# Modulation vectors of the second FFN: summed around the attention in place of the FFNs before it

## The chip, the cores and the metric

The kernel runs on one core of one Trainium2 chip. The metric is the device time of one execution in microseconds (us). The engines are TensorE (PE in the profile; its weight loads are PEld), VectorE (DVE), ScalarE (ACT), GpSimd (POOL) and SyncE (SP), which here only issues transfers. Each engine runs its own list of instructions in the order in which the built program holds it.

## The reference

Two layers with shared structure act on 640 tokens (512 latent, 128 context) of width 1024. A layer is a half-step FFN, an attention block and another half-step FFN. Every one of the three is modulated by vectors that come from a linear map of the condition:

```
ada = (silu(c) @ w_ada[l] + b_ada[l])             # 9 vectors of 1024 for latent, 9 for context tokens
sh1, sc1, g1, sh2, sc2, g2, sh3, sc3, g3 = split(ada, 9)
x = x + 0.5*g1 * ((silu(h @ w_gate) * (h @ w_up)) @ w_down)      # h = rmsnorm(x)*(1+sc1)+sh1
x = x + g2 * (concat(o_mla, o_diff, o_nat) @ w_out)              # attention, from ONE input product h @ w_in
x = x + 0.5*g3 * ((silu(h @ w_gate2) * (h @ w_up2)) @ w_down2)   # h with sc3, sh3
```

Vectors are numbered 0 to 8 per layer. Numbers 6, 7 and 8 (sh3, sc3, g3) belong to the second FFN of the layer, 3, 4 and 5 to the attention.

## The kernel before, in words

**Stages.** `build` runs, for each of the two layers, `ffn(l, "f1")`, `attention(l)` and `ffn(l, "f2")`. Activations lie transposed, a tile of 128 features by 640 tokens. All products are made in three passes (high part by high part, high by low, low by high), so each weight block must be split first: ScalarE casts the high part, VectorE subtracts to get the low part (`Stream.split`). An FFN makes two pairs of blocks plainly, then ten pairs of gate and up blocks by a seven-product scheme (`seven`), with the down products in five chunks between them.

**The order of the work.** The kernel records instructions in Python program order; a scheduler then orders each engine's list by that order and by the readiness that it models. In the attention a planner (`Plan`, with `Clock`) chooses between chains (scores, softmax, outputs) and bulk work (input products `feat` and `tokmm`) by modelled ready times. The first bulk work is nq0, nk0 and nv0 for token group 0 (columns 0 to 383), then for group 1 (384 to 639). Results land in PSUM banks; a product of `feat` takes one of the two banks of tag `q`, and takes it only when the readers of its last content are done. For nq0 and nk0 the readers are ScalarE's cast and VectorE's subtraction (`split` in `attention`).

**The boundary before the attention.** At the end of `ffn(l, "f1")` the norm of group 0 and of group 1 is applied (`Boundary.norm`, `Norm.apply`): per feature block a multiply by the broadcast norm, a scale and shift, a cast and the subtraction for the low part, mostly on VectorE. That stands right ahead of the attention's first products.

**The background work.** `Background` sums the modulation vectors. A step takes one vector, one of eight feature blocks and one half of the 1024 inputs: a load of 256 KB from `in_ADA` into a tile of 128x512, and two `tensor_tensor_reduce` on VectorE, one for each of the conditions (`ada_step`). In the profile such a reduce is `CUSTOM_DVE_ANT_0` followed by `DVE_READ_ACCUMULATOR2_ANT part<-`; in the instruction order it reads `ISA ... part<-` followed by `ISA part 128x1`. A vector is 16 steps, hence 32 reduces. `open(limit, rate)` puts the vectors up to `limit` on the list, sets the rate, and loads four rows of the condition through SiLU. `tick` adds the rate to a credit and makes a step for each whole unit. An FFN ticks after each of the seven products and each down product; the very first FFN also ticks three times after each plain product (`EARLY`). `require(l, v)` makes steps at once until vector v is there; it stands ahead of the first down product (vector 2 or 8) and at each boundary (the scale). `finish()` makes all steps that are left, at once. It is called in one place, the first line of `attention`:

```
    def attention(l, bound, nbound):
        BG.finish()
```

Of the kernel before, what the change touches and what calls it, by code (L numbers as in the profile page):

```python
# [51 lines left out]

FETCH = 5
EARLY = 3
RATES = 0.517, 0.339, 0.423, 0
LIMITS = (0, 8), (1, 3), (1, 8), (1, 8)

UNITS = "nnnnnnnnddddddddmmmmmmmm"

# [130 lines left out]
class Clock:  # L190
# [42 lines left out]
    def bank(self, tag, tile):  # L233
        b = self.banks[tag]
        if len(b) >= self.BUFS[tag]:
            b.remove(min(b, key=lambda n: self.used.get(n, 1e18)))
        b.append(tile.tensor.name)
        return tile
# [40 lines left out]
class Plan:  # L279
# [18 lines left out]
    def done(self, name):  # L298
        return not self.open.get(name)
# [28 lines left out]
def build(tc, I, O):  # L328
# [31 lines left out]
    def PB(n=512):  # L360

        return clock.bank("q", pp.tile([128, n], F32, tag="q", name=nm("q"), bufs=4 - NP))
# [123 lines left out]
    def mm3(out, a, b, start, stop, skip=False):  # L486
        PE.matmul(out, a[0], b[0], start=start, stop=False, skip_group_check=skip)
        PE.matmul(out, a[0], b[1], start=False, stop=False, skip_group_check=skip)
        PE.matmul(out, a[1], b[0], start=False, stop=stop, skip_group_check=skip)
# [79 lines left out]
    BG = Background()  # L569
# [133 lines left out]
    def hcols(hT, k, c0, c1):  # L703
        return hT[k][0][:, c0:c1], hT[k][1][:, c0:c1]
# [166 lines left out]
    def attention(l, bound, nbound):  # L871
# [21 lines left out]
        def feat(tag, g, name, done):  # L893
            yield ("q",)
            ps = PB(GR[g][1] - GR[g][0])
            for k in range(ND):
                mm3(ps, W.get((l, tag, k)), hcols(hT, k, *GR[g]), k == 0, k == ND - 1)
                yield
            follow(name, done(ps))

        def tokmm(tag, j, width, name, done, bank=PB):
            yield ("q",) if bank is PB else ()
            ps = bank(width)
            for k in range(ND):
                wh, wl = W.get((l, tag, k))
                hh, hl = hcols(hT, k, j * 128, (j + 1) * 128)
                PE.matmul(ps, hh, wh, start=(k == 0), stop=False)
                PE.matmul(ps, hl, wh, start=False, stop=False)
                PE.matmul(ps, hh, wl, start=False, stop=(k == ND - 1))
                yield  # L910
            follow(name, done(ps))

        def follow(name, chain):
            if chain is not None:
                plan.chain(chain, name)
# [32 lines left out]
        def ckv(j):  # L948
            def done(ps):
                if j == 0:  # L950
                    M["kr"] = pu.tile([128, 5, 32], F32, tag="kr", name=nm("kr"), bufs=1)
                    M["ck"], M["ckP"] = HL(), (PQ("ck", F32R), PQ("ck", F32R))
                    M["mc"] = T(256)
                    SP.dma_start(M["mc"], I["mctx"][l])
                A.copy(M["kr"][:, j], ps[:, 128:160])
                if j == 4:
                    plan.chain(kr_rope(), "ckv")
                return post(rms_rows(ps[:, 0:128], 128))

            def post(t):  # L960
                yield (t, "p")
                pt = P1((128,))
                PE.transpose(pt, t, ident)
                h, lo = hcols(M, "ck", 128 + j * 128, 256 + j * 128) if j < 4 else M["ckP"]
                A.activation(h, pt, AF.Identity, scale=kvn(l))
                V.scalar_tensor_tensor(lo, pt, kvn(l), f32(h), ALU.mult, ALU.subtract)
                if j == 4:
                    o = T(128)
                    V.tensor_scalar(o, pt, kvn(l), None, ALU.mult)
                    G.dma_start(O["ckvT"][l], o)  # L970
                    split(M["ck"][0][:, 0:128], M["ck"][1][:, 0:128], M["mc"][:, 0:128])

            return tokmm("ckv", j, 160, "ckv", done)

        def cq(j):
            def done(ps):
                if j == 0:
                    cqT[0], cqT[1] = HL(), HL()
                return post(rms_rows(ps, 256))

            def post(t):
                yield (t, "p")
                pt = P1((2, 128))
                for c in range(2):
                    PE.transpose(pt[:, c], t[:, c * 128:(c + 1) * 128], ident)
                for c in range(2):
                    h, lo = hcols(cqT, c, j * 128, (j + 1) * 128)
                    A.activation(h, pt[:, c], AF.Identity, scale=qn(l, c))
                    V.scalar_tensor_tensor(lo, pt[:, c], qn(l, c), f32(h), ALU.mult, ALU.subtract)

            return tokmm("cq", j, 256, "cq", done)
# [47 lines left out]
        def nq(i, g):  # L1039
            def done(ps):  # L1040
                if g == 0:
                    Qn[i] = HL(S)
                    split(Qn[i][0][:, 0:384], Qn[i][1][:, 0:384], ps, NAT_SCALE)
                else:
                    split(Qn[i][0][:, 384:512], Qn[i][1][:, 384:512], ps[:, 0:128], NAT_SCALE)
                    QPn[i] = PQ(("n", i))
                    A.activation(QPn[i], ps[:, 128:256], AF.Copy, scale=NAT_SCALE)
            return feat(f"nq{i}", g, f"n{i}", done)

        def nk(i, g):  # L1050
            def done(ps):
                if g == 0:
                    K = Kn[i] = HL()
                    split(K[0][:, 0:256], K[1][:, 0:256], ps[:, 0:256])
                    split(K[0][:, 384:512], K[1][:, 384:512], ps[:, 256:384])
                    split(K[0][:, 256:384], K[1][:, 256:384], nkc[:, i * 128:(i + 1) * 128])
                else:
                    K = Kn[i]
                    split(K[0][:, 512:640], K[1][:, 512:640], ps[:, 0:128])
                    KPn[i] = PQ(("n", i))  # L1060
                    A.copy(KPn[i], ps[:, 128:256])
                    G.dma_start(O["nkT"][l, i], KPn[i])
            return feat(f"nk{i}", g, f"n{i}", done)
# [329 lines left out]
        def dqk(tag, t, g):  # L1393
            def done(ps):
                if g == 0:
                    M[tag, t] = T()
                xf = M[tag, t]
                A.copy(xf[:, GR[g][0]:GR[g][1]], ps)
                if g == 0:
                    return  # L1400
                del M[tag, t]
                y = rope(xf)
                pq = PQ(("d", t))
                A.copy(pq, xf[:, 512:640])
                if tag == "dq":
                    hl = HL(S)
                    split(hl[0], hl[1], y, DIFF_SCALE)
                    QPd[t] = pq
                else:
                    hl = HL()  # L1410
                    split(hl[0][:, 128:640], hl[1][:, 128:640], y)
                    split(hl[0][:, 0:128], hl[1][:, 0:128], M["dc"][:, t * 128:(t + 1) * 128])
                    KPd[t] = pq
                    G.dma_start(O["dkT"][l, t], pq)
                M[tag, "hl", t] = hl
            return feat(f"{tag}{t}", g, f"d{t}", done)
# [263 lines left out]
    def first(k):  # L1680
        for d in range(k + 1 if k else 0, min(k + 2, ND)):
            begin(d)
        if k == ND - 1:
            for e in engines:
                e.pin = None
            W.la = LA["ffn"]
            BG.open(LIMITS[0], RATES[0])

# [3 lines left out]
    def lambdas():  # L1692
        for l in range(L):
            li = 0.8 - 0.6 * math.exp(-0.3 * l)
            pr = SM(2)
            tt = T(64).rearrange("p (a k) -> p a k", a=2)
            lv = lamv[:, l].rearrange("p (a b) k -> p a b k", a=2)
            tc.keep_in_program_order(V.tensor_tensor(tt, lv[:, :, 0], lv[:, :, 1], ALU.mult))
            V.tensor_reduce(pr, tt, AX.X, ALU.add)
            A.activation(pr, pr, AF.Exp)  # L1700
            V.tensor_tensor(neglam[:, l:l + 1], pr[:, 1:2], pr[:, 0:1], ALU.subtract)
            V.tensor_scalar(neglam[:, l:l + 1], neglam[:, l:l + 1], -li, None, ALU.add)
            V.tensor_scalar(subg[:, l:l + 1], sub(l), 1.0 - li, None, ALU.mult)

    for l in range(L):
        b2 = Boundary(l, "mix")
        if l:
            BG.open(LIMITS[2], RATES[2])
        ffn(l, "f1", b, b2, None if l else first)
        if l == 0:  # L1710
            lambdas()
        b3 = Boundary(l, "f2")
        attention(l, b2, b3)
        b = Boundary(l + 1, "f1") if l + 1 < L else Boundary(l, "final")
        BG.open(LIMITS[2 * l + 1], RATES[2 * l + 1])
        ffn(l, "f2", b3, b)
# [125 lines left out]
```

## Time and profile before

| | us |
|---|---|
| median of 3 runs | 2736.33 (2736.01 to 2740.82) |
| profiled execution, its own time | 2733.88 |
| span of the profiled execution | 2732.1 |
| PE busy | 2566.5 (94%) |
| PEld busy | 2429.6 (89%) |
| DVE busy | 2019.7 (74%) |
| ACT busy | 1202.0 (44%) |
| POOL busy | 592.9 (22%) |

By the tile names in the timeline, the first FFN lasts to about 525 us, the first attention to about 940, the second FFN to about 1400, the third FFN to about 1850, the second attention to about 2270 and the last FFN to the end. PE's share of 94% is a mean over stages in which it is busy nearly all the time and stretches in which it waits.

### The profile page before, as it was taken

The page shows a single profiled execution, that of the slowest core. Times are in us where ns is not written, and L with a number is a line of the kernel's source. Part 1 is how long each engine was busy: PE and PEld are TensorE (multiplying, and loading weights), DVE is VectorE, ACT ScalarE, POOL GpSimd, SP SyncE. Part 2 cuts the span into 40 slices and gives each one's busy share as a digit, 9 for nine tenths or more (in the row PEclk, how much of TensorE's full clock was granted, in tenths as well). Part 3 has the DMA queues.
Part 4 walks back from the last instruction along what each step waited for, and adds up shares of the span by engine and source line. Part 5 has one row for each costly group of instructions (what it writes and reads, how often), then busy time and mean ns, then how long its engine had stood idle before and what let it go on. Part 6 is the DMA issues. An engine that isn't in the chain of part 4 may idle for free. (4 is left out here: it accounts for less than half of the span.)

```text
span 2732.1 us, 46623 instructions
## 1 busy us (share of the span) xinstructions
PE 2566.5 (94%) x17216; PEld 2429.6 (89%) x17216; DVE 2019.7 (74%) x4542; ACT 1202.0 (44%) x2618; POOL 592.9 (22%) x618
## 2 busy tenths in 40 slices
PE   5799999999989999999999999999988898999998
PEld 5799999977867899999999999998777788999998
DVE  4999999633476799888779999965345669666665
ACT  4333334454366553333453333335445666333441
POOL 0322222012223122222112222301122312222220
PEclk9899999999989999999999999999999899999999
DMA  6376666221321346665436665632213212545441
GB/s 243 119 207 197 199 199 172 95 88 58 93 53 42 117 131 182 172 172 163 140 78 185 197 177 165 182 103 79 89 54 90 54 63 80 144 122 137 123 120 39
DMA packets 144819, 349.73 MB, mean 128 GB/s; under 512 B 18496, under 2 KB 21472, under 8 KB 144592
## 3 DMA queue, kind: packets, MB, share of 16 engines
q1 hardware_dynamic: 119616, 302.28, 34.1%
q0 software_dynamic: 23392, 42.97, 9.6%
q8 instruction: 136, 2.23, 0.3%
q10 hardware_dynamic: 1584, 1.50, 0.2%
q14 instruction: 91, 0.75, 0.1%
HBM read 330.27 MB, written 4.36 MB: 122 GB/s over the span
## 5 line engine op out<-in xcount | busy, mean ns | idle before, releaser
L272 PE MATMUL q<-t,u 128*128 128x320 f32 (+2 forms) x8448 | 1369.3, 315 | 42.9 <-DVE t L272 27.8
L272 PEld LDWEIGHTS q<-t,u 128*128 128x128 f32 x8448 | 1272.2, 191 | 72.8 <-issue 26.0
L272 DVE TENSOR_TENSOR u<-raw,u 128x512 fp32r<-128x512 f32 (+1 forms) x668 | 489.1, 738 | 126.5 <-ACT u L272 80.6
L272 ACT CAST u<-raw 128x512 fp32r<-128x512 f32 (+1 forms) x668 | 400.7, 616 | 362.3 <-PE q L272 150.5
L272 PE MATMUL s<-t,u 128*128 128x320 f32 (+2 forms) x3008 | 515.7, 323 | 24.5 <-ACT u L272 9.2
L272 PEld LDWEIGHTS s<-t,u 128*128 128x128 f32 (+1 forms) x3008 | 450.9, 192 | 44.6 <-ACT t L272 10.5
L272 PE MATMUL p<-t,u 128*128 128x320 f32 (+1 forms) x2936 | 458.8, 315 | 6.0 <-DVE v L272 5.8
L272 PEld LDWEIGHTS p<-t,u 128*128 128x128 f32 (+1 forms) x2936 | 427.4, 186 | 19.5 <-issue 8.6
L272 DVE CUSTOM_DVE_ANT_0 u<-u,u 128x512 f32<-128x512 f32 x512 | 393.0, 771 | 15.8 <-PE q L272 6.1
L272 DVE SCALAR_TENSOR_TENSOR t<-q,adav,t 128x192 f32<-128x192 f32 (+3 forms) x568 | 235.1, 436 | 118.2 <-PE q L272 117.6
L272 POOL TENSOR_TENSOR u<-raw,raw 128x512 f32<-128x512 f32 x78 | 131.5, 1685 | 474.0 <-PE q L272 149.0
L272 ACT CAST u<-u 128x512 fp32r<-128x512 f32 x234 | 144.8, 619 | 194.8 <-PE q L272 83.0
L272 DVE TENSOR_TENSOR u<-u,u 128x512 fp32r<-128x512 f32 (+2 forms) x265 | 194.1, 732 | 43.2 <-PE q L272 11.8
L272 ACT ACTIVATE t<-t 128x320 f32<-128x320 f32 (+2 forms) x168 | 92.4, 553 | 183.5 <-DVE t L272 180.0
L272 POOL DMA_DIRECT2D raw<-in_W x78 | 68.7, 880 | 476.8 <-DVE t L272 186.3
L272 PE MATMUL q<-u,t 128*128 128x256 f32 (+1 forms) x1086 | 152.9, 298 | 18.8 <-ACT u L272 11.5
L272 PEld LDWEIGHTS q<-u,t 128*128 128x128 f32 x1086 | 143.1, 203 | 24.4 <-ACT u L272 13.5
L272 ACT CAST t<-t 128x320 fp32r<-128x320 f32 (+3 forms) x155 | 78.4, 544 | 104.3 <-DVE t L272 102.8
L272 POOL TENSOR_TENSOR u<-u,raw 128x512 f32<-128x512 f32 x78 | 120.3, 1542 | 17.5 <-DVE u L272 7.4
L272 POOL DMA_DIRECT2D u<-in_W x78 | 76.7, 983 | 188.0 <-DMA u<-in_W 54.6
L272 POOL TENSOR_TENSOR sm<-sm,mhalf 128x1 f32<-128x1 f32 (+5 forms) x37 | 33.1, 895 | 380.7 <-DVE sm L272 379.2
L272 DVE TENSOR_TENSOR v<-p,v 128x320 f32<-128x320 f32 x195 | 94.1, 483 | 20.5 <-PE p L272 19.5
(168 smaller groups left out, 2080.3 us busy)
## 6 DMA issues: line engine op xcount, KB each, us to landing
raw<-in_W SPq DMA_DIRECT2D x330, 512.0 KB, 4.0
u<-in_ADA SPq DMA_DIRECT2D x272, 256.0 KB, 4.5
u<-in_W SPq DMA_DIRECT2D x78, 256.0 KB, 4.2
raw<-in_W POOLq DMA_DIRECT2D x78, 256.0 KB, 5.1
u<-in_W POOLq DMA_DIRECT2D x78, 256.0 KB, 5.8
t<-t SPq DMA_DIRECT2D x80, 80.0 KB, 2.1
t<-in_nbias SPq DMA_DIRECT2D x16, 320.0 KB, 5.0
u<-u SPq DMA_DIRECT2D x80, 64.0 KB, 2.0
```

The lines of the kernel that those rows point to most:

```text
L272: r = f(*a, **k)
```

## The change

The limits and rates of the two FFNs that come first in their layer are lowered, so that vectors 6, 7 and 8 of each layer are no longer summed in them. A second table, `BETWEEN`, opens these vectors just before `attention` is called, at 0.2 steps per tick, and the loops of `feat` and `tokmm` in the attention tick once for each of their eight slices.

```
-RATES = 0.517, 0.339, 0.423, 0
-LIMITS = (0, 8), (1, 3), (1, 8), (1, 8)
+RATES = 0.3, 0.339, 0.17, 0
+LIMITS = (0, 5), (1, 3), (1, 5), (1, 8)
+
+BETWEEN = ((0, 8), 0.2), ((1, 8), 0.2)
 ...
             for k in range(ND):                      # feat
                 mm3(ps, W.get((l, tag, k)), hcols(hT, k, *GR[g]), k == 0, k == ND - 1)
+                BG.tick()
                 yield
 ...
                 PE.matmul(ps, hh, wl, start=False, stop=(k == ND - 1))     # tokmm
+                BG.tick()
                 yield
 ...
         b3 = Boundary(l, "f2")
+        BG.open(*BETWEEN[l])
         attention(l, b2, b3)
```

Per layer three vectors move: 48 steps, 96 reduces, 48 loads. The number of steps in all stays.

How the instructions stand. First VectorE's list of the kernel before, at the boundary to the first attention. `p_5992` is the broadcast norm of group 1, `v` and `t` are the tiles of its application, `q_6077` and `q_6106` are the banks of the first two input products (nq0 and nk0, group 0), and `raw` rows are weight splits:

```order
L272 TENSOR_SCALAR v_5989<-ident,sm_5986 128x128 x2
L272 SCALAR_TENSOR_TENSOR u_6103<-q_6077,u_6102 128x384
L272 TENSOR_TENSOR v_5994<-p_5992,t_75 128x256
L272 TENSOR_TENSOR u_6153<-raw_5693,u_6152 128x512
L272 TENSOR_SCALAR v_5995<-v_5994,adav_91 128x128
L272 TENSOR_TENSOR v_6001<-p_5992,t_76 128x256
L272 TENSOR_TENSOR u_6165<-raw_6162,u_6164 128x512
L272 TENSOR_TENSOR t_5729<-v_5995,t_5728 128x256
L272 TENSOR_SCALAR v_6002<-v_6001,adav_91 128x128
L272 TENSOR_TENSOR v_6008<-p_5992,t_77 128x256
L272 TENSOR_TENSOR t_6132<-q_6106,t_6131 128x256
```

The same place now, where the banks of the first two products are `q_6089` and `q_6118`:

```order
L274 TENSOR_SCALAR v_5741<-ident,sm_5738 128x128 x2
L274 TENSOR_TENSOR v_5746<-p_5744,t_75 128x256
L274 TENSOR_SCALAR v_5747<-v_5746,adav_91 128x128
L274 TENSOR_TENSOR v_5753<-p_5744,t_76 128x256
L274 TENSOR_SCALAR v_5754<-v_5753,adav_91 128x128
L274 ISA u_5836,part<-u_5830,u_5818 128x512
L274 ISA part 128x1
L274 TENSOR_TENSOR t_5481<-v_5747,t_5480 128x256
L274 TENSOR_TENSOR v_5760<-p_5744,t_77 128x256
L274 TENSOR_TENSOR t_5489<-v_5754,t_5488 128x256
L274 TENSOR_SCALAR v_5761<-v_5760,adav_91 128x128
L274 TENSOR_TENSOR v_5767<-p_5744,t_78 128x256
```

The readers of the two banks and the two weight splits have left this place, and the first reduce stands in it. All 96 reduces of the layer follow within 224 rows, with the rest of the norm and the eight small rows of `lambdas` between the first of them. After the last reduce VectorE's list goes on so:

```order
L274 ISA u_6064,part<-u_6064,u_5821 128x512
L274 ISA part 128x1
L274 TENSOR_TENSOR t_6144<-q_6118,t_6143 128x256
L274 TENSOR_TENSOR adav_91<-part 128x16
L274 TENSOR_TENSOR adav_91<-adav_91,bada 128x16
L274 TENSOR_SCALAR adav_91<-adav_91 128x16
L274 TENSOR_TENSOR t_6144<-q_6118,t_6143 128x128
L274 TENSOR_TENSOR t_6144<-u_6078,t_6143 128x128
L274 SCALAR_TENSOR_TENSOR u_6115<-q_6089,u_6114 128x384
L274 TENSOR_TENSOR u_6165<-raw_5445,u_6164 128x512
```

The two readers of bank `q_6118`, the reader of `q_6089` and the next weight split now stand behind the 96th reduce. The second layer's list has the same shape at its own boundary: the reader rows of the first two banks stand behind its 96th reduce.

Then TensorE's list now, at the third product that takes a bank of tag `q` (`q_6240`, nq0 for group 1); `s_1262` is a bank of nv0:

```order
L274 MATMUL s_1262_6213<-u_5448,t_5512 128x256
L274 MATMUL s_1262_6213<-u_5447,t_5520 128x256
L274 MATMUL s_1262_6213<-u_5447,t_5521 128x256
L274 MATMUL s_1262_6213<-u_5448,t_5520 128x256
L274 MATMUL q_6240<-t_5480,u_5325 128x256
L274 MATMUL q_6240<-t_5481,u_5325 128x256
L274 MATMUL q_6240<-t_5480,u_5326 128x256
```

In the kernel before, the same product (there `q_6228`) stands behind more work on nv0:

```order
L272 MATMUL s_1258_6201<-u_6152,t_5777 128x256
L272 MATMUL s_1258_6201<-u_6153,t_5776 128x256
L272 MATMUL s_1258_6201<-u_6152,t_5784 128x256
L272 MATMUL s_1258_6201<-u_6152,t_5785 128x256
L272 MATMUL s_1258_6201<-u_6153,t_5784 128x256
L272 MATMUL q_6228<-t_5728,u_5573 128x256
L272 MATMUL q_6228<-t_5729,u_5573 128x256
```

Between the broadcast of the group 1 norm and this product TensorE's list holds 14 products of nk0 and 52 of nv0 before, and 14 and 16 now; the other 36 follow it now. Beyond such places TensorE's list holds the same products in the same order, and GpSimd's list is the same row for row.

## Rows read from the trace of the kernel before

**Rows 1.** The page: the span, then busy time, share and instructions of each engine.

```profile
span 2732.1 us, 46623 instructions
...
PE 2566.5 (94%) x17216; PEld 2429.6 (89%) x17216; DVE 2019.7 (74%) x4542; ACT 1202.0 (44%) x2618; POOL 592.9 (22%) x618
```

**Rows 2.** Windows: stretch, length, PE, PEld, DVE, ACT, POOL busy (count), PEclk, DMA, GB/s.

```profile
100.00:150.00 50.00, 35.66 (x222) 33.96 (x221) 48.76 (x116) 17.47 (x39) 10.94 (x11) 0.86 0.41 128
150.00:450.00 300.00, 292.82 (x1969) 288.46 (x1969) 296.88 (x695) 104.08 (x194) 77.30 (x64) 1.00 0.68 194
...
550.00:750.00 200.00, 185.89 (x1279) 158.93 (x1278) 73.41 (x213) 91.28 (x263) 41.84 (x76) 0.97 0.25 80
1000.00:1350.00 350.00, 345.42 (x2334) 342.12 (x2334) 311.94 (x672) 133.54 (x244) 84.68 (x70) 1.00 0.60 173
...
1450.00:1800.00 350.00, 341.85 (x2300) 338.54 (x2299) 328.24 (x732) 130.65 (x239) 85.65 (x70) 1.00 0.64 181
2310.00:2660.00 350.00, 350.00 (x2389) 350.00 (x2388) 240.48 (x432) 144.00 (x260) 92.20 (x74) 1.00 0.48 127
```

**Rows 3.** The page's costliest groups: the reduces of the modulation vectors.

```profile
L272 DVE CUSTOM_DVE_ANT_0 u<-u,u 128x512 f32<-128x512 f32 x512 | 393.0, 771 | 15.8 <-PE q L272 6.1
```

**Rows 4.** Timeline of VectorE (start, length): four reduces in a row, and what follows.

```profile
122.20 0.68 DVE L272 CUSTOM_DVE_ANT_0 u<-u,u 128x512 f32<-128x512 f32 x1
...
124.65 0.48 DVE L272 TENSOR_TENSOR v<-q,v 128x320 f32<-128x320 f32 x1
```

**Rows 5.** Timeline of VectorE: one of the long reduces.

```profile
316.70 1.79 DVE L272 CUSTOM_DVE_ANT_0 u<-u,u 128x512 f32<-128x512 f32 x1
```

**Rows 6.** Timeline of GpSimd at the time of that reduce.

```profile
316.30 1.63 POOL L272 TENSOR_TENSOR u<-u,raw 128x512 f32<-128x512 f32 x1
```

**Rows 7.** Timeline of VectorE at the start of the first attention.

```profile
534.47 0.42 DVE L272 TENSOR_TENSOR v<-p,t 128x256 f32<-128x256 f32 x1 [0.33 <-PE p L272]
...
536.94 0.34 DVE L272 TENSOR_SCALAR v<-v,adav 128x128 f32<-128x128 f32 x1
537.20 0.41 DVE L272 TENSOR_TENSOR v<-p,t 128x256 f32<-128x256 f32 x1
537.53 0.41 DVE L272 TENSOR_TENSOR t<-q,t 128x256 fp32r<-128x256 f32 x1
...
540.88 0.42 DVE L272 TENSOR_TENSOR t<-v,t 128x256 fp32r<-128x256 f32 x1
541.22 0.34 DVE L272 TENSOR_SCALAR v<-v,adav 128x128 f32<-128x128 f32 x1
```

**Rows 8.** Timeline of TensorE at the start of the first attention.

```profile
534.08 2.80 PE L272 MATMUL q<-t,u 128*128 128x384 f32 x14
536.72 6.63 PE L272 MATMUL s<-u,t 128*128 128x256 f32 x52
543.19 2.08 PE L272 MATMUL q<-t,u 128*128 128x256 f32 x16
```

**Rows 9.** Timeline of TensorE at the start of the second attention.

```profile
1863.04 6.63 PE L272 MATMUL s<-u,t 128*128 128x256 f32 x52
1869.51 5.92 PE L272 MATMUL q<-t,u 128*128 128x256 f32 x48
```

**Rows 10.** Timeline of VectorE there: the first multiply of group 1's norm.

```profile
1860.79 0.42 DVE L272 TENSOR_TENSOR v<-p,t 128x256 f32<-128x256 f32 x1 [0.33 <-PE p L272]
```

**Rows 11.** The tile in_ADA: its loads, and time from issue to landing.

```profile
L272 SPq DMA_DIRECT2D u<-in_ADA x272: 327/328/1206, 8.7 to 1759.9; - x136
...
DMA to landing us min/median/max: 2.6/4.5/9.0
```

**Rows 12.** Timeline of TensorE after a wait of 9.24 us.

```profile
121.80 0.90 PE L272 MATMUL s<-t,u 128*128 128x320 f32 x2 [9.24 <-ACT u L272]
...
125.78 3.03 PE L272 MATMUL s<-t,u 128*128 128x320 f32 x10 [2.82 <-DVE u L272]
```

**Rows 13.** Windows, as in rows 2: three us after that wait.

```profile
122.00:125.00 3.00, 0.96 (x3) 0.58 (x3) 3.00 (x10) 0.26 (x1) 0.00 (x0) 0.50 0.00 0
```

More of the change, by code (lines that the diff above doesn't have):

```diff
@@ L54 @@
 EARLY = 3
-RATES = 0.517, 0.339, 0.423, 0
-LIMITS = (0, 8), (1, 3), (1, 8), (1, 8)
+RATES = 0.3, 0.339, 0.17, 0
+LIMITS = (0, 5), (1, 3), (1, 5), (1, 8)
+BETWEEN = ((0, 8), 0.2), ((1, 8), 0.2)
 UNITS = "nnnnnnnnddddddddmmmmmmmm"
@@ L897, in feat @@
                 mm3(ps, W.get((l, tag, k)), hcols(hT, k, *GR[g]), k == 0, k == ND - 1)
+                BG.tick()
                 yield
@@ L909, in tokmm @@
                 PE.matmul(ps, hh, wl, start=False, stop=(k == ND - 1))
+                BG.tick()
                 yield
@@ L1712, in build @@
         b3 = Boundary(l, "f2")
+        BG.open(*BETWEEN[l])
         attention(l, b2, b3)
```

## The prediction

> **What bounds the kernel now.** I began with the page's busy times: TensorE is busy for 94% of a span of 2732.1 us and VectorE for 74% [rows 1]. Such a mean hides the stages, so next I cut the span into stretches of single stages [rows 2]. The last FFN sums no modulation vectors: 2389 matmuls in 350 us, 0.1465 us each, without a gap. That is TensorE at its own pace, and the yardstick for the other FFNs. The second FFN (0.339 steps a tick) makes 2334 in 350 us, 55 fewer or 8.1 us lost; the third (0.423) makes 2300, 13.0 us lost; the first (0.517) makes 1969 in 300 us where the pace allows 2048, 11.6 us lost, and 222 in the 50 us before that where 341 would fit, 17.4 us lost. VectorE is busy for 89%, 94% and 99% of the three long stretches. So TensorE bounds all FFNs, and a full VectorE costs them a little. In the attention VectorE is busy for 73.4 of 200 us [rows 2]: there is room in it, if the work is spread. Then I read the timelines at the head of the two attentions, where the order shows the moved reduces.
>
> **What is added: a block of reduces ahead of the readers.** The ticks put into the attention find nothing to do: its first line, finish(), makes all 48 steps before the first input product is recorded, and the order shows the result, 96 reduces on VectorE ahead of the rows that empty the first two `q` banks. TensorE's third product into such a bank (nq0, group 1) cannot start until the second reader of `q_6118` is done, and everything behind it on TensorE waits with it. The cost is that idle time, once per layer.
>
> Where TensorE stops: in before, 14 products of nk0 start at 534.08 and the nv0 products at 536.72 [rows 8]. Now 16 of the 52 stand ahead of the blocked product; at 6.63/52 = 0.1275 us each they end at 536.72 + 2.0 = 538.8.
>
> Where it goes on: VectorE starts on the group 1 norm at 534.47 [rows 7]. From there to the releasing row it has:
> - the norm: eight times a multiply (537.20 to 537.53, 0.33), a scale and shift (536.94 to 537.20, 0.26) and a subtraction (540.88 to 541.22, 0.34), 0.93 each, 7.4 us;
> - 96 reduces. Four of them in a row with their accumulator reads take from 122.20 to 124.65, 0.6125 us each [rows 4], 58.8 us. The mean over all 512 is 0.771 us [rows 3], which would be 74.0;
> - the tail: the two readers (the longer one 0.41 [rows 7]), ScalarE's cast between them and three short adav rows, together some 1.0 us, my estimate from that row.
>
> 534.47 + 7.4 + 58.8 + 1.0 = 601.7. Idle: 601.7 - 538.8 = 62.9 us. In the second layer the norm starts at 1860.79 [rows 10] and TensorE stops at 1863.04 + 2.0 = 1865.1 [rows 9]; 1860.79 + 67.2 = 1928.0, again 62.9 us.
>
> Why 0.6125 and not 0.771: the mean holds reduces such as one of 1.79 us [rows 5] which stood beside a GpSimd addition of two tiles at 316.30 [rows 6]. GpSimd's list has no such addition between the norm and the first softmax, so the block has nothing to share with. The Trainium skill ("SBUF — State Buffer", on the shared port pair) says that a VectorE instruction with two SBUF inputs and a GpSimd instruction that reads SBUF exclude each other for a whole instruction. The trace agrees at 316 us. By that rule the block goes at the undisturbed pace; without it I would have to take the mean, 30 us more over both layers.
>
> After the idle time TensorE's clock: after a wait of 9.24 us the granted clock is 0.50 from 122 to 125 us [rows 13], the 1.2 GHz level, and ten matmuls take 3.03 us, 0.303 each where 0.1465 is the full pace [rows 12]. These ten and the two before them lose 12 x 0.156 = 1.9 us; I take 2.0 after each block.
>
> Sum of what is added: 2 x (62.9 + 2.0) = 129.8 us. Its lower bound is what is worked out here, since no row has a faster reduce; its upper bound is the mean, 2 x 15.2 = 30.4 us more.
>
> **Loads.** The 48 loads of each layer move too, from SP's list in the FFN to the boundary, ahead of the loads for context keys, rotary tables and biases. A load is issued when a buffer comes free, and in the order that is nine to ten reduces before the first reduce that needs it: 9 x 0.6125 = 5.5 us, against a landing of 4.5 us in the median, 2.6 to 9.0 [rows 11]. At 0.6125 us a reduce the block asks for 256 KB in 1.225 us, 214 GB/s; 194 GB/s is what the first FFN moves over 300 us with PE and VectorE busy [rows 2]. So the loads keep up, with little to spare; I cost them at nothing, and if that cover fails the price is the rival below. The four condition rows and their SiLU on ScalarE, twice, start under the last FFN products and the group 0 norm and are hidden there.
>
> **What is removed.** 96 reduces leave the first FFN and 96 the third. A stall of TensorE goes, and what is late next is nothing: the last FFN shows that without these reduces splits and results keep pace. Losses by rate: 0 at rate 0, 8.1 us in 350 at 0.339. Linear between: rate 0.17 loses 4.1 us, so the third FFN gains 13.0 - 4.1 = 8.9. Rate 0.3 loses 8.1 x 0.30/0.339 x 300/350 = 6.1 us in the first FFN's long stretch: gain 11.6 - 6.1 = 5.5. In the 50 us before, the splitting of the norm's blocks is the main load, and require() before the first down product still forces vector 2: 16 steps by then, where 37 ticks (ten plain products at three, seven of `seven`) at 0.517 made 19. Three steps, six reduces, about 3 us. Together 17.4 us. Bounds: 0, and all that the three stretches lose, 17.4 + 11.6 + 13.0 = 42.0. (That the first two numbers agree is chance.)
>
> **Sum.** 129.8 - 17.4 = +112.4 us. The profiled execution took 2733.88 us, 1.8 more than its span; 2733.9 + 112.4 = 2846.3. The median of the runs is 2.4 above the profiled execution, so I say 2848.
>
> **The rivals.**
> - The block is fed too slowly. If a load takes 7 us from issue to use, between the median and the longest [rows 11], nine reduces take 7 us, 0.78 each: 192 x (0.78 - 0.6125) = 32 us more, 2880. For it: the spare time is 1 us, and a landing of 9.0 is on record. Against it: the 4.5 us were taken beside the weight stream, which is mostly still in the block. Chance 0.20.
> - VectorE was the true bound of the first and third FFN: all 42.0 us come back, 2848 - 24.6 = 2823. For it: 99% and 94%. Against it: the second FFN at 89% still loses 8.1, so part of the loss goes with any rate. Chance 0.12.
> - The other side: faster, by the words of the change. The reduces would fill VectorE's free time in the attention (126.6 of 200 us [rows 2]) and TensorE would not wait: 2736 - 17.4 = 2719. That needs the readers of the two banks to run before the block, so either another order than the one that stands there or a VectorE that passes over it. The idle time decides: under 8.7 us per layer (17.4/2) the kernel is not slower. The Trainium skill ("TensorE: Matmul & The Clock Gate", on the array and the engines' queues) calls VectorE's queue strictly first in, first out; no run here shows that apart from the order. Chance 0.04.
>
> **How the numbers follow.** Forecast 0.64, with 2830 to 2866 as its own range (its loads some 0.05 us a reduce slower, its gain 5 to 30). The range 2822 to 2882 leaves out most of the third rival and the upper part of the first, about 0.15. A difference within 0.2%, about 5.5 us, is what a measurement of this kernel can't tell from none; forecast and the first two rivals are slower by far more. Slower 0.96, same 0.01, faster 0.03.
>
> **What would show it.** In the profile after: at each attention's head a stretch of some 60 us in which VectorE runs only `part` reduces, 0.61 us from start to start, GpSimd still, and TensorE idle with VectorE's `t` as releaser, then a stretch at half clock. Pairs of reduces with idle time before them, released by in_ADA, would speak for the first rival. The third FFN's middle 350 us should hold some 2360 matmuls; 2389 would speak for the second. Reduces spread between softmax rows, and no idle of TensorE at the head, would make the prediction wrong.

## The result, and the profile after

The changed kernel takes 2850.99 us (median of 4 runs, 2843.41 to 2855.74), the kernel before 2736.17 us beside it (2733.34 to 2740.82): ratio 1.0435, 95% interval 1.0411 to 1.046. The forecast was 2848 with a range of 2822 to 2882, slower. The profiled execution took 2848.73 us (span 2847.0; TensorE's mean granted clock, as a share of its full 2.4 GHz, 0.952 against 0.974).

First the timeline of TensorE after (start, length, engine, line, operation, out<-in, shape, count, and in brackets the idle time before it with its releaser): the first FFN, the heads of both attentions, and the multiplies `p<-v,ones` by which the stages can be marked.

```profile
148.58 16.69 PE L274 MATMUL q<-t,u 128*128 128x320 f32 x95 [12.44 <-DVE t L274]
...
525.53 0.70 PE L274 MATMUL p<-v,ones 128*128 128x256 f32 x2 [0.39 <-DVE v L274]
...
528.50 2.07 PE L274 MATMUL s<-u,t 128*128 128x256 f32 x16
595.61 1.40 PE L274 MATMUL q<-t,u 128*128 128x256 f32 x5 [65.05 <-DVE t L274]
596.82 6.45 PE L274 MATMUL s<-u,t 128*128 128x256 f32 x36
...
989.83 0.81 PE L274 MATMUL p<-v,ones 80*128 80x320 f32 x2 [0.59 <-DVE v L274]
...
1908.16 0.70 PE L274 MATMUL p<-v,ones 128*128 128x256 f32 x2 [0.39 <-DVE v L274]
...
1977.46 1.41 PE L274 MATMUL q<-t,u 128*128 128x256 f32 x5 [64.27 <-DVE t L274]
1978.67 5.45 PE L274 MATMUL s<-u,t 128*128 128x256 f32 x36
...
2377.26 0.81 PE L274 MATMUL p<-v,ones 80*128 80x320 f32 x2 [0.58 <-DVE v L274]
```

Where [rows 8] show 52 products of nv0 in one piece and no idle time, TensorE now makes 16, then stands for 65.05 us, and for 64.27 us in the second layer [rows 9]. The same marks in the kernel before:

```profile
533.73 0.70 PE L272 MATMUL p<-v,ones 128*128 128x256 f32 x2 [0.39 <-DVE v L272]
...
933.96 0.81 PE L272 MATMUL p<-v,ones 80*128 80x320 f32 x2 [0.59 <-DVE v L272]
...
1860.05 0.70 PE L272 MATMUL p<-v,ones 128*128 128x256 f32 x2 [0.39 <-DVE v L272]
...
2263.17 0.81 PE L272 MATMUL p<-v,ones 80*128 80x320 f32 x2 [0.58 <-DVE v L272]
```

From mark to mark, the first stage counted from the start of the span and the last to its end:

| us | first FFN | attention 1 | second and third FFN | attention 2 | last FFN |
|---|---|---|---|---|---|
| before | 533.7 | 400.2 | 926.1 | 403.1 | 468.9 |
| after | 525.5 | 464.3 | 918.3 | 469.1 | 469.7 |
| difference | -8.2 | +64.1 | -7.8 | +66.0 | +0.8 |

The sum is +114.9, the difference of the spans. The prediction had -8.5, +64.9, -8.9, +64.9 and 0.

VectorE's timeline shows what the idle time is filled with: the start of the norm, the first reduce, two in the middle and the last, and the rows behind it.

```profile
526.26 0.42 DVE L274 TENSOR_TENSOR v<-p,t 128x256 f32<-128x256 f32 x1 [0.79 <-PE p L274]
...
527.70 0.68 DVE L274 CUSTOM_DVE_ANT_0 u<-u,u 128x512 f32<-128x512 f32 x1
...
569.60 0.68 DVE L274 CUSTOM_DVE_ANT_0 u<-u,u 128x512 f32<-128x512 f32 x1
...
570.21 0.68 DVE L274 CUSTOM_DVE_ANT_0 u<-u,u 128x512 f32<-128x512 f32 x1
...
593.74 0.68 DVE L274 CUSTOM_DVE_ANT_0 u<-u,u 128x512 f32<-128x512 f32 x1
...
594.35 0.42 DVE L274 TENSOR_TENSOR t<-q,t 128x256 fp32r<-128x256 f32 x1
...
595.18 0.28 DVE L274 TENSOR_TENSOR t<-q,t 128x128 fp32r<-128x128 f32 x1
```

The reduces follow each other at 0.61 us, as in [rows 4]; the two readers `t<-q` stand behind the last of them, and TensorE goes on when the second is done. Windows after (columns as in [rows 2]; the stretch of the third FFN lies as far from its mark as that of before):

```profile
100.00:150.00 50.00, 29.36 (x160) 27.82 (x159) 46.38 (x102) 17.05 (x38) 13.10 (x12) 0.80 0.41 126
150.00:450.00 300.00, 299.49 (x2025) 298.66 (x2025) 260.75 (x554) 113.33 (x205) 74.22 (x63) 0.99 0.58 161
540.00:600.00 60.00, 4.39 (x20) 4.42 (x21) 57.40 (x194) 2.63 (x7) 0.00 (x0) 0.50 0.69 212
595.60:598.60 3.00, 2.99 (x14) 3.00 (x15) 1.86 (x4) 1.08 (x3) 0.00 (x0) 0.50 0.67 215
1498.00:1848.00 350.00, 347.93 (x2359) 347.32 (x2359) 276.90 (x552) 138.31 (x251) 84.67 (x72) 1.00 0.56 153
```

In the block VectorE is full, GpSimd still and the granted clock 0.50; in the first 3 us behind the wait it is 0.50 still, the 1.2 GHz level. The third FFN makes 2359 matmuls instead of 2300, the long stretch of the first 2025 instead of 1969; the 50 us before it make 160 instead of 222.

### The profile page after: what moved, and what is told of

The parts are those of the page before. It is cut to its first block, busy times and chain, and to the rows that moved or that the text cites. A ratio compares the mean times of both kernels' runs of the same rounds, so it can differ in the third digit from the quotient of the medians.

```text
span 2847.0 us, 46668 instructions
## 1 busy us (share of the span) xinstructions
PE 2559.9 (90%) x17216; PEld 2429.9 (85%) x17216; DVE 2030.5 (71%) x4542; ACT 1211.5 (43%) x2626; POOL 588.9 (21%) x618
## 5 line engine op out<-in xcount | busy, mean ns | idle before, releaser
L274 DVE TENSOR_TENSOR u<-raw,u 128x512 fp32r<-128x512 f32 (+1 forms) x668 | 497.9, 751 | 156.1 <-ACT u L274 86.1
L274 PEld LDWEIGHTS p<-t,u 128*128 128x128 f32 (+1 forms) x2936 | 429.7, 186 | 15.0 <-issue 7.4
L274 DVE CUSTOM_DVE_ANT_0 u<-u,u 128x512 f32<-128x512 f32 x512 | 357.0, 721 | 30.4 <-PE q L274 17.0
L274 DVE TENSOR_TENSOR u<-u,u 128x512 fp32r<-128x512 f32 (+2 forms) x265 | 202.3, 763 | 58.6 <-ACT u L274 20.6
```

Source lines behind the costliest of these rows:

```text
L274: r = f(*a, **k)
```

## The experiments

Theory: the loss is the block of 96 reduces ahead of the bank readers, and lasts as long as VectorE needs for them; the FFNs give back 16 us. Rivals: the loads set its pace; it is slowed by a shared port; the reduces cost TensorE as much wherever they stand in the attention. "Head" below means the first `p<-v,ones` of an attention.

| run | us, median | ratio to before | first FFN | att. 1 | second, third FFN | att. 2 |
|---|---|---|---|---|---|---|
| e1_no_finish | 2763.67 | 1.0118 (1.0096 to 1.0140) | 527.1 | 429.7 | 919.4 | 423.6 |
| e2_no_vectors | 2720.26 | 0.9960 (0.9941 to 0.9979) | 527.7 | 393.7 | 923.1 | 403.6 |
| e3_few_loads | 2847.49, one run | | 524.5 | 464.7 | 921.8 | 463.9 |
| e4_half_reduces | 2801.20, one run | | 526.4 | 441.6 | 920.0 | 442.0 |
| e5_thin_spread | 2751.45 | 1.0077 (1.0051 to 1.0102) | 528.2 | 423.7 | 910.6 | 420.2 |
| e6_late_start | 2754.49 | 1.0080 (1.0052 to 1.0108) | 525.2 | 411.0 | 927.3 | 417.9 |
| e7_pool_beside | 2881.07, one run | | 525.7 | 479.6 | 920.2 | 484.4 |
| e8_one_vector | 2745.53 | 1.0048 (1.0028 to 1.0068) | 531.1 | 411.3 | 927.8 | 400.0 |
| e9_early5 | 2842.87, one run | | 518.4 | 466.4 | 917.8 | 469.2 |
| e10_late_layer0 | 2740.21 | 1.0034 (1.0020 to 1.0047) | 520.7 | 413.8 | 931.2 | 393.3 |
| e11_late_two | 2735.15 | 1.0028 (1.0014 to 1.0043) | 527.9 | 400.0 | 928.8 | 401.2 |

The stages come from one profiled execution each. How far they may be trusted: the second attention of before, e10 and e11 is built from the same source, with TensorE's products in the same order, and took 403.1, 393.3 and 401.2 us. Windows over whole attentions (columns as in [rows 2]) show what differs: the second attention of before and of e10, then the first of before, of e11 and of e1.

```profile
1860.05:2263.17 403.12, 370.45 (x2437) 316.10 (x2438) 211.26 (x520) 217.53 (x574) 86.84 (x134) 0.94 0.24 72
1865.71:2258.97 393.26, 360.00 (x2438) 306.71 (x2438) 210.90 (x520) 217.48 (x574) 86.83 (x134) 0.97 0.24 74
533.73:933.96 400.23, 367.44 (x2437) 313.93 (x2438) 212.03 (x528) 217.77 (x576) 86.85 (x134) 0.95 0.24 73
527.91:927.90 399.99, 361.87 (x2437) 308.65 (x2438) 255.41 (x662) 219.86 (x580) 88.82 (x134) 0.97 0.30 94
527.09:956.77 429.68, 379.40 (x2437) 322.37 (x2437) 276.16 (x728) 220.12 (x580) 89.87 (x134) 0.92 0.31 97
```

In the second attention TensorE's idle time (the length less its busy time) is 32.7 us in before and 33.3 in e10, but the same products kept it busy for 370.5 and 360.0 us, at a granted clock of 0.94 and 0.97. So the length of an attention can differ by 10 us with the granted clock alone, and the idle time is the better measure of what reduces cost there. The first FFN is the same in the changed kernel and in e1 to e7, and took 524.5 to 528.2 us. The profiled executions of e10 and e11 (2731.98 and 2729.39 us) are also the fastest of their runs, so their stages sum to less than those of any other of their runs would.

**e3_few_loads, the loads.** Of vectors 6 to 8 only three loads a layer are made and read again by all 96 reduces, so that none can wait for a load; the sums are then not those of the weight.

```
+            if self.steps[0][1] > 5:
+                if not self.kept:
+                    self.kept = [ada_load(*self.steps[i]) for i in range(3)]
+                s = self.steps.pop(0)
+                ada_step(*s, self.kept[len(self.steps) % 3], self.rows, T(512))
 ...
```

> The changed kernel, but of the 48 loads of each block only three are made, and their buffers are read again by all 96 reduces (the vectors 6 to 8 thus don't come from their own rows of the weight; everything else is as it was). Nothing can wait for a load in the block. Theory (VectorE's own time sets the block, 0.6125 us a reduce, and the loads are covered): idle of TensorE 62 to 65 us per layer as in the changed kernel, time 2845 to 2852. Rival (the block is fed by loads or slowed by their traffic): reduces below 0.60 us from start to start, idle shorter by more than 5 us per layer, time below 2840.

Measured: 2847.49 us, TensorE's timeline at the head:

```profile
595.03 2.69 PE L274 MATMUL q<-t,u 128*128 128x256 f32 x11 [65.49 <-DVE t L274]
```

65.49 us idle without the loads, 65.05 with them. The loads did not set the block's pace: the rival of the prediction that priced it at 2880 is out.

**e4_half_reduces, the number of reduces.** Of each step of vectors 6 to 8 the second reduce is left out, and its half of the sum counts as 0; the loads stay.

```
 ...
-        for i in range(2):
+        for i in range(1 if v > 5 else 2):
```

> The changed kernel, but of vectors 6 to 8 only one of the two reduces of each step is made (the other half of the sum is left out and counts as 0), with all the loads as they are. Theory (idle time = number of reduces ahead of the readers x 0.6125): 48 reduces fewer per layer, 29.4 us less idle time, 34 to 37 us per layer, time 2851 - 59 = 2792. Rival (the loads set the block's pace: 48 loads of 256 KB per layer): they moved at 212 GB/s beside the full block; if that is their limit, 12.6 MB take 59 us still, the idle time stays near 60 us with VectorE waiting for loads between reduces, time 2840 or above. Between: a new limit of the loads shows once the block asks for 428 GB/s; then idle 40 to 55 us, with in_ADA as VectorE's releaser.

Measured: 2801.20 us. TensorE's timeline:

```profile
543.49 4.70 PE L274 MATMUL q<-t,u 128*128 128x256 f32 x24 [12.07 <-DVE t L274]
572.84 0.58 PE L274 MATMUL q<-t,u 128*128 128x256 f32 x1 [24.65 <-DVE u L274]
573.22 6.70 PE L274 MATMUL s<-u,t 128*128 128x256 f32 x36
```

12.07 + 24.65 = 36.72 us idle, 28.3 less than 65.05; 48 x 0.6125 = 29.4 were expected. So the idle time is the number of reduces by their duration. The time is 9 us over the expected 2792: the order now lets the readers of one bank through, the idle time falls into two pieces, and TensorE restarts below its pace twice per layer (24 products in 4.70 us, at a mean granted clock of 0.61, where [rows 9] have 48 in 5.92). The block also comes to the edge of its loads here, in VectorE's timeline and in a window:

```profile
546.52 0.69 DVE L274 CUSTOM_DVE_ANT_0 u<-u,u 128x512 f32<-128x512 f32 x1 [0.73 <-DMA u<-in_ADA]
```

```profile
545.00:570.00 25.00, 3.20 (x19) 2.99 (x18) 21.87 (x70) 0.00 (x0) 0.00 (x0) 0.57 0.99 352
```

With one reduce a load it moves 352 GB/s at a DMA share of 0.99, and VectorE stands for 3.1 of the 25 us; the full block moved 212 at 0.69.

**e7_pool_beside, the shared port.** The prediction took 0.6125 us and not the mean of 0.771 [rows 3] because GpSimd is still in the block.

```
+        x, y = T(512), T(512)
+        G.memset(x, 1.0)
+        for i in range(24):
+            G.tensor_tensor(y, x, x, ALU.add)
         BG.finish()
```

> The changed kernel with 24 added GpSimd additions of two tiles (128x512, on scratch tiles that nothing uses) per attention, issued ahead of the block of reduces; nothing else is changed. Theory (such an addition and a reduce with two SBUF inputs shut each other out, as at 316 us of the kernel before, where a reduce took 1.79 us beside an addition of 1.63): each addition that falls into the block lengthens it by about 1 us; with all 24 in it 24 us per layer, idle 85 to 90 us instead of 65, reduces near 1.2 us or more from start to start beside the additions, time 2870 to 2900. Rival (the long reduce at 316 us had another cause and the two engines do not disturb each other): reduces 0.6125 us from start to start, idle 65, time 2845 to 2855.

Measured: 2881.07 us. The timelines of GpSimd, VectorE and TensorE:

```profile
524.28 29.85 POOL L274 TENSOR_TENSOR u<-u 128x512 f32<-128x512 f32 x24
```

```profile
544.23 1.32 DVE L274 CUSTOM_DVE_ANT_0 u<-u,u 128x512 f32<-128x512 f32 x1
...
545.49 1.25 DVE L274 TENSOR_TENSOR t<-v,t 128x256 fp32r<-128x256 f32 x1
546.66 1.06 DVE L274 TENSOR_SCALAR v<-v,adav 128x128 f32<-128x128 f32 x1
547.64 0.41 DVE L274 TENSOR_TENSOR v<-p,t 128x256 f32<-128x256 f32 x1
...
551.38 0.68 DVE L274 CUSTOM_DVE_ANT_0 u<-u,u 128x512 f32<-128x512 f32 x1
```

```profile
610.98 1.41 PE L274 MATMUL q<-t,u 128*128 128x256 f32 x5 [80.63 <-DVE t L274]
```

The two engines do shut each other out: a reduce takes 1.32 us instead of 0.68, a subtraction 1.25 instead of 0.43, a scale and shift 1.06 instead of 0.34, while the row that reads its first input from PSUM (`v<-p,t`) stays at 0.41. The Trainium skill ("SBUF — State Buffer", "SBUF: two separate sides") says this of VectorE instructions with two SBUF inputs or in a two-port mode, against GpSimd instructions that read SBUF; the rows agree, though none shows which of the two holds for the scale and shift. The idle time grew by 15.6 us and not by the 24 expected: the additions fell mostly beside the norm, each held up one VectorE row by 0.64 to 0.82 us (24 of them make 15 to 20 us), the reduce at 551.38 is back at 0.68, and with the last addition over at 554.13 the rest of the block goes at full pace.

**e2_no_vectors, the gain by itself.** Vectors 6 to 8 are left out altogether and set to 0.

```
-        BG.open(*BETWEEN[l])
+        BG.todo = [t for t in BG.todo if t[0] != l or t[1] < 6]
+        G.memset(adav[l][:, 6:9], 0.0)
+        BG.done.update((l, v) for v in (6, 7, 8))
```

> The changed kernel, but modulation vectors 6 to 8 of each layer are not summed at all: they are set to 0 by GpSimd, and neither their loads nor their 192 reduces are made, in the attention or elsewhere. The rates of the FFNs are those of the changed kernel. That leaves the gain of the FFNs alone. Theory (gain 16 to 17.4): 2736 - 16 = 2720, range 2712 to 2726, attentions at 399 to 400 us as before. Rival (VectorE was the true bound of the first and third FFN, all 42 us come back, and something else in the changed kernel costs some 25 us): 2694 to 2705. Rival (no gain in the FFNs): 2733 or above.

Measured: 2720.26 us; 0.0040 x 2731 = 10.9 us faster than before (5.7 to 16.1). That is below the 16 of the stage table and the 17.4 of the prediction, but holds the first in its interval. 42 us are out. In its profile 9.1 us lie in the FFNs (6.1 and 3.0) and 6.5 in the first attention, where TensorE idles for 33.9 us, no less than before, at a granted clock of 0.97: the gain of the FFNs themselves may be nearer 9 us than 16.

**e1_no_finish, spread reduces.** One line goes, and the ticks do what the change's words say.

```
     def attention(l, bound, nbound):
-        BG.finish()
```

> The changed kernel without the call of finish() at the head of the attention, so that the ticks among the input products make the 48 steps of the layer. In the order they then stand spread over the first half of the attention, some 30 reduces per 100 rows of VectorE. Theory (the block ahead of the bank readers is the whole loss, 2 x about 65 us, and the FFNs gave back 16): no idle time of TensorE over 8 us with VectorE as releaser at the attention's head; the 58.8 us of reduces fit into VectorE's free time there (before: busy 80 of the first 200 us, 131 of the next 200), so each attention takes between 399.5 us as before and 410; 2851 - 130 = 2721, up to 2740 if the spread reduces delay readers. Rival (the reduces cost TensorE about their own time wherever they stand in the attention, by memory or by the queue): the attentions stay near 460 us and the kernel near 2850. Rival (half): the ticks come too seldom or too late and a rest is forced at the attention's end: idle there, 2750 to 2800.

Measured: 2763.67 us, 87 less than the changed kernel and 32 more than before. The block is most of the loss, but the theory's 2721 to 2740 failed: the attentions took 429.7 and 423.6. TensorE (it waits 8.09 us at the head) and VectorE in the first attention:

```profile
540.22 5.61 PE L274 MATMUL q<-t,u 128*128 128x256 f32 x30 [8.09 <-DVE u L274]
...
558.25 1.49 PE L274 MATMUL s<-t,u 64*128 64x384 f32 x12
...
567.11 0.96 PE L274 MATMUL s<-t,u 64*128 64x512 f32 x6 [3.66 <-DVE sm L274]
```

```profile
565.39 0.69 DVE L274 CUSTOM_DVE_ANT_0 u<-u,u 128x512 f32<-128x512 f32 x1
...
566.01 0.55 DVE L274 CUSTOM_DVE_ANT_0 u<-s,t 128x384 f32<-128x384 f32 x1
```

The scores of 558.25 are there by 559.74, yet VectorE's first row on them (`u<-s,t`) starts at 566.01, behind a piece of 19 reduces in its list. The windows above give the price: in the first attention TensorE's idle time grew from 32.8 to 50.3 us, and its products took 379.4 us instead of 367.4, at a granted clock of 0.92. So free time of VectorE over 200 us is not room for reduces: its list is served in order, and softmax rows wait behind whatever stands in front of them.

**e5_thin_spread and e6_late_start.** Both without `finish()`:

```
-BETWEEN = ((0, 8), 0.2), ((1, 8), 0.2)
+BETWEEN = ((0, 8), 0.125), ((1, 8), 0.125)           # e5; e6: 0.1334
 ...
-        BG.finish()
 ...
         BG.open(*BETWEEN[l])
+        BG.credit = -4.0                             # e6 alone
```

> No call of finish() at the attention's head, as in e1_no_finish, but the rate among the input products is 0.125 a tick instead of 0.2 (392 ticks per attention, so the 48 steps last almost to its end). In VectorE's order the largest piece of reduces without other work falls from 19 to 11, with two of 8 and 7. Theory A (what is left of the loss in e1, some 25 us per attention, comes from pieces of reduces that stand ahead of softmax and reader rows in VectorE's list, and thinner pieces cost less): attentions 405 to 415 us against 400 and 403 before, time 2730 to 2748. Theory B (each reduce in an attention costs TensorE about 0.26 us, 25/96, wherever it stands): attentions as in e1, 2758 to 2768. Theory C (the attention's later half is worse, VectorE is busier there: 131 of 199 us against 80 of 200): above 2770.

> As e5_thin_spread, but the first 30 ticks of each attention make no step (credit starts at -4) and the rest run at 0.1334, so that the steps still end with the attention. It keeps the reduces away from the readers of the first q banks, where e1 had a wait of TensorE of 8.1 us. If the head is what costs (theory H): that wait is gone in both layers, and the time is 8 to 16 us under e5_thin_spread. If only the density counts (theory A): within 4 us of e5_thin_spread, since the later pieces grow a little.

Measured: 2751.45 and 2754.49 us. Thinner pieces cost less than in e1 (12 us), and the attentions still took 23 and 17 us more than before in e5, 11 and 15 in e6: theory A in direction, not in size. In e6 the wait at the head is gone in both layers and the first attention is 12.6 us shorter than in e5, but the second and third FFN are 17 us longer, and the time is the same. So H holds for the head and not for the kernel. Split at the `p<-v,ones` of the norm between the two FFNs (1393.46 us in e5, 1388.20 in e6), 10.3 us of it lie in the second FFN, which took 451.9 us in e6, 441.6 in e5, 446.3 in the changed kernel and 443.7 before, at the same rate in all four. Why it differs the runs don't show.

**e8_one_vector.** Vector 8 alone among the attention's products.

```
+RATES = 0.45, 0.339, 0.33, 0
+LIMITS = (0, 7), (1, 3), (1, 7), (1, 8)
+
+BETWEEN = ((0, 8), 0.045), ((1, 8), 0.045)
 ...
-        BG.finish()
```

> No finish() at the attention's head, and only vector 8 of each layer is summed among the attention's input products (16 steps, 32 reduces, 0.045 a tick); vectors 6 and 7 go back to the FFNs (limits 7 instead of 5, rates 0.45 and 0.33). 48 steps per attention cost 23 and 17 us in e5_thin_spread and 11 and 15 in e6_late_start, 17 in the mean, and took 7.5 and 5.6 us (means of five profiles) from the FFNs. Theory A (cost grows with the density, so that a third of the steps costs far less than a third): attentions within 2 us of 400 and 403, FFNs some 4 us shorter, time 2726 to 2732 beside 2730 for before: a version that is not slower, maybe a little faster. Theory B (a fixed price per reduce): 5 to 6 us per attention, less 4 from the FFNs: 2736 to 2740, slower than before by 0.2 to 0.4%.

Measured: 2745.53 us, above both theories. TensorE and VectorE at the first head:

```profile
541.93 3.75 PE L274 MATMUL q<-t,u 128*128 128x256 f32 x16 [5.76 <-ACT t L274]
```

```profile
538.50 0.68 DVE L274 CUSTOM_DVE_ANT_0 u<-u,u 128x512 f32<-128x512 f32 x1
...
541.24 0.55 DVE L274 SCALAR_TENSOR_TENSOR u<-q,u 128x384 fp32r<-128x384 f32 x1
```

Two reduces stand in the norm, and TensorE stops after 16 products of nv0, at 536.18. The reader of the first bank (541.24) stands behind the norm and the 36 other products of nv0 behind the product of group 1, as in the changed kernel, so nothing covers the norm: TensorE waits 5.76 us, until the reader ends at 541.79 and ScalarE's last cast of the norm beside it (which of the two decided, the rows don't tell), and restarts at the lower clock (0.50 from 542 to 545 us) with 16 products in 3.75 us. The second attention has no such wait and took 400.0. So the head is priced by the order that the recorded steps bring about, more than by their number.

**e9_early5, the forced steps.**

```
-EARLY = 3
+EARLY = 5
```

> The changed kernel with EARLY = 5 instead of 3: the ten early products of the first FFN then make 17 steps at the rate 0.3 before require() asks for vector 2, so that no steps are forced ahead of the first down product (the changed kernel forces five there, ten reduces, 6.1 us). If the forced steps cost TensorE (its wait of 12.4 us at 148 us and the 160 matmuls between 100 and 150 us, against 222 in the kernel before): more than 200 matmuls there, the head of the first attention 3 to 6 us earlier than 525.5. If it is the sum of the reduces before that point that counts, whenever they stand: the wait only moves, the head within 2 us of 525.5, time 2846 to 2853.

Measured: 2842.87 us, the head at 518.35, 7.2 us earlier than in the changed kernel, a little more than the 3 to 6 expected. Windows:

```profile
100.00:150.00 50.00, 37.44 (x240) 36.53 (x240) 48.46 (x109) 18.00 (x40) 12.19 (x12) 0.86 0.40 123
150.00:450.00 300.00, 298.47 (x2030) 297.45 (x2030) 264.54 (x555) 117.00 (x210) 77.97 (x65) 1.00 0.60 166
```

240 matmuls instead of 160, and no wait ahead of the first down product. The forced steps did cost TensorE.

**e10_late_layer0 and e11_late_two, a version that beats both.** e9's first FFN with e6's late steps in layer 0, layer 1 as before; then the same with vector 6 back in the first FFN.

```
+EARLY = 5                                            # e11: 3.8
+RATES = 0.3, 0.339, 0.423, 0                         # e11: 0.36 first
+LIMITS = (0, 5), (1, 3), (1, 8), (1, 8)              # e11: (0, 6) first
+
+BETWEEN = (0, 8), 0.1334                             # e11: 0.1
 ...
-        BG.finish()
 ...
-        BG.open(*BETWEEN[l])
+        if l == 0:
+            BG.open(*BETWEEN)
+            BG.credit = -4.0
```

> A version put together from the runs before: in layer 0 the first FFN of the changed kernel with EARLY = 5 (e9_early5: head of the first attention 15.4 us earlier than in the kernel before) and the 48 steps among the attention's input products after 30 ticks (e6_late_start: 411.0 us against 400.2); in layer 1 everything as in the kernel before (limits 8, rate 0.423, nothing in the second attention). Theory (the prices add: -15.4 + 10.8 = -4.6): 2724 to 2730 beside 2730 to 2732 of before, attention 1 at 411, no wait over 3 us at its head. Rival (what the first FFN gives is taken back behind the attention, as in e6_late_start, whose second and third FFN took 927.3 us where the changed kernel took 918.3): 2732 to 2740.

> As e10_late_layer0, but vector 6 goes back to the first FFN (limit 6, rate 0.36, EARLY 3.8) and the attention sums vectors 7 and 8 alone (32 steps, 0.1 a tick, after 40 ticks; largest piece 6 reduces instead of 9). If the attention's price falls faster than the first FFN's gain (density): attention 1 at 403 to 406, the first FFN 8 to 12 us shorter than in before, time 2722 to 2728, under e10_late_layer0. If both go in proportion: within 3 us of e10_late_layer0. If the rate in the first FFN has a threshold between 0.3 (2030 matmuls in 300 us) and 0.45 (1965): FFN gain 3 us, time 2730 to 2735.

Measured: 2740.21 and 2735.15 us. Both lie within 0.35% of before, and above it: 1.0034 and 1.0028, with intervals that leave out 1 and overlap each other, so that e11 is not shown to be the better of the two. In e10 the first FFN kept 13.0 us, the first attention cost 13.6 and the second and third FFN 5.1. In e11 the first FFN kept 5.8 us and the first attention took 400.0, but not because its reduces were free: by the windows above TensorE idles there for 38.1 us instead of 32.8, and the granted clock of this execution (0.97 against 0.95) made up for it. The profile is itself faster than the one of before (span 2727.6); the median of the runs keeps none of it. No version I ran that sums all the vectors is faster than the kernel before.

## Why the prediction was right

- **The block ahead of the readers.** Shown: idle 65.05 and 64.27 us where 62.9 was worked out. The formula (norm, 96 x 0.6125, tail) gave 66.2 from the norm's start to the last reduce's end; the rows have 68.1 (526.26 to 594.35). The 1.9 us are the rows between the reduces that I had left out: finished vectors, the rows of `lambdas`, one wait of 0.34. With the restart the block cost 67.7 us in layer 0, where the attention is 64.1 longer: 3.6 us came back later in it (the granted clock was 0.71 from 810 to 830 us before, and 0.87 on about the same products, 869 to 889, after). That the two attentions came within 1.1 us of the 64.9 forecast is in part luck. e4 takes half the reduces and 28.3 us of idle time away, e1 takes the block and 87 us of the time.
- **0.6125 and not 0.771 us.** Shown: 0.61 in the block; e7 puts GpSimd beside VectorE, and a reduce takes 1.32.
- **Restart at half clock, 2.0 us.** At the pace of before (0.1275 us for nv0 [rows 8], 0.1233 for q [rows 9]) the 5 and 36 products after the wait lost 0.8 + 1.9 = 2.6 us in layer 0 and 0.8 + 0.9 = 1.7 in layer 1; mean 2.1.
- **Loads at nothing.** Shown by e3 (65.49 against 65.05). Their median landing is 3.3 us after, 4.5 before [rows 11]:

```profile
u<-in_ADA SPq DMA_DIRECT2D x272, 256.0 KB, 3.3
```

- **Third FFN, 8.9 us.** "Some 2360 matmuls" were forecast and 2359 came: 59 x 0.1465 = 8.6 us. By the marks the third FFN alone is some 10 us shorter (472.0 against 482.4); the stage of the table gained 7.8, since the second FFN, whose rate did not change, is 2.6 longer.
- **First FFN, 5.5 + 3.** The sum was right (8.2 for 8.5) by luck: both terms were wrong, to opposite sides. The failed step is "Three steps, six reduces, about 3 us": 37 ticks at the new rate of 0.3 make 11 steps, and 16 are wanted, so `require()` makes five at once, ten reduces, ahead of the first down product. That is the wait of 12.44 us at 148.58 (1.6 us of it VectorE itself stands for a load) and the 160 matmuls. Matched by product, TensorE starts its 900th at 161.85 us before and at 166.58 after: 4.7 us lost there, not 3 gained. e9 shows the cause: with 17 steps made in time the 900th starts at 158.19, 3.7 us ahead of before, and the head comes 7.2 us earlier than in the changed kernel. From there to the 3000th product (485.36 before, 477.15 after) the changed kernel gained 12.9 us instead of 5.5; in the window of 300 us that is 56 x 0.1465 = 8.2. The loss is not in proportion to the rate: the full pace would be 2048, 0.3 makes 2025 and 2030, 0.36 makes 2000 (e11), and 0.45 makes 1965 (e8), no better than 0.517 (1969).
- **The rival on the other side** had its condition right (the block must go) and its price wrong: it saw 126.6 free us of VectorE in 200 and took spread reduces as hidden. e1 is slower than before by 32 us, not faster by 17. With the order it asked for, the change still loses.

Open: why the second FFN, at one rate in all, took from 441.6 us (e5) to 451.9 (e6), and why the granted clock of an attention differs between executions. In e10 and e11 the third FFN has the rate of before, so no gain was due there.

## What to carry to other kernels

Work moved "among" other work goes where the order puts it: look for the call that flushes the queue, and read the order before the rates. An engine's free time is no room for background work where its list also carries the rows that the bottleneck waits for; there the size of the pieces and their place in the list count beside the sum (e1, e5 and e6 make the same reduces). And a lower rate with an unchanged deadline turns into a burst at the deadline.

## What was not expected of the hardware

- Beside 24 GpSimd additions VectorE and GpSimd alternated row by row: 24 additions in 29.85 us, a VectorE row with SBUF inputs for each; the row that reads PSUM was not held up.
- The transfers of this block reached 352 GB/s at a DMA share of 0.99, and VectorE then waited for a load of 256 KB by up to 0.73 us in the first layer's block and 1.54 in the second's.
- In the second attention of before and e10, with the same products and the same idle time within 0.6 us, the granted clock was 0.94 and 0.97, and the time differed by 10 us.
